# Decay masks of an SSD scan made by TensorE, with sums and products moved from POOL to DVE

## The chip, the cores and the metric

The kernel runs on one core of a Trainium2 chip. The metric is the device time of one execution in microseconds (us). Before the change it is 2617.65 us, the median of three runs (2610.93 to 2621.97).

The core has a matrix engine (PE in the profile, with its weight loads as PEld), a vector engine (DVE), an activation engine (ACT), a general engine (POOL) and a queue engine (SP), each of which works through its own list of instructions in order. [...] 

## The reference, cut to what matters

One encoder layer over 256 + 1024 tokens (1280 columns here), model width 1024, fp32. A projection gives the input of an S5 branch, of a bidirectional Mamba-2 (SSD) branch, and gates. Both branches are merged, projected, added to x, and a squared-ReLU MLP of width 4096 follows. The SSD branch has 24 heads of 64 in 4 groups, state 128, chunks of 128 tokens; it runs forward (d = 0) and backward (d = 1):

```python
da_cs = jnp.cumsum(dt * a, axis=2)                       # within a chunk
decay = jnp.exp(jnp.where(lower, da_cs[l] - da_cs[s], -jnp.inf))
cb = einsum('bclgn,bcsgn->bclsg', cm, bm)
y_diag = einsum('bclsg,bclsgk,bcsgkp->bclgkp', cb, decay, x * dt)
chunk_states = einsum('bcsgn,bcsgk,bcsgkp->bcgkpn', bm, decay_in, x * dt)
prev = scan: carry * chunk_decay + chunk_states
y_off = einsum('bclgn,bcgkpn,bclgk->bclgkp', cm, prev, jnp.exp(da_cs))
y = y_diag + y_off + d_skip * x;  out = rmsnorm_by_group(y * silu(z)) * w
```

For every pair (s, l) of a chunk and every head the kernel needs the weight dt[s] exp(cs[l] - cs[s]) in the lower triangle for one direction, in the upper for the other, times cb.

## The kernel before, in words

Activations lie with features on the partitions and the 1280 tokens along the free axis. Products of full precision are made as three fp32r matmuls (high and low parts of weights and inputs, mm3 at L129 and mm3n at L138) on 128x128 weight tiles over column chunks of 512, 512 and 256. Weights come over SP, are split by ACT (wh, L113) and POOL (wl, L114).

The order of the work on each engine is fixed when the kernel is built: a scheduler takes the instructions by priority (the order of the code, with parts marked urgent ahead) and by its own idea of when each is ready, and waits are then put in. So projection tiles that stand later in the code fill PE between the steps of earlier work.

The stages: input norm and projection of u; S5; the projection tiles EARLY (gates, conv and z tiles of group 0); dt_proc (L350 on); LATE (conv and z tiles of group 1); then the SSD with groups j = 0 to 3 and chunks k = 0 to 9, with the tiles of groups 2 and 3 and the last gates (TAIL) as fill; the GLU of S5; merge, output projection; MLP; final norm.

dt_proc computes dt (v), its sums within a chunk (e), and factors for the states (f) as 128x640 tiles (rows: half, direction, head). It writes e to the DRAM scratch cs_d in 16 stores and turns e, v and f by 15 PE transposes to per-token columns (ncs, dtt, dst).

chunk_in (L470) loads xf, transposes it (xt, L477), and advances the backward state (next_state, L447: POOL multiplies by dec, L454, PE makes the increment, L449, DVE adds, L456). chunk_out (L515) does one chunk of one group: SP loads bc and xz; PE makes cb (L523), DVE masks it twice (L525). ACT's queue loads ec, e broadcast over 64 partitions per head (L531), and ACT takes its exponential (L540); PE makes the off-diagonal products with the states (L538) in the banks ba and bk, DVE multiplies (L541), POOL adds the directions (L544). For each half of the six heads, ACT's queue loads cr, both directions' e broadcast over 128 partitions (L550); ACT subtracts the column's own e for direction 0 (L553), DVE does it for direction 1 and takes the minimum (L556), ACT takes the exponential (L558); ACT and DVE make the weight w of the two masked cb and dt (L561, L562), and DVE multiplies (L563). PE makes y (L568); DVE adds the skip (L571), POOL the off part and the gate (L573, L574); SP stores yt (L575); ACT squares (L578), POOL sums the squares (L579, L580).

PSUM in this stage: mm 2 banks, ps 2, ba 2, bk 1, y 1. The lines of the profile are those of the functions below.

Of the kernel before, what the change touches and what calls it, by code (L numbers as in the profile page):

```python
# [8 lines left out]
F32 = mybir.dt.float32  # L9
F32R = mybir.dt.float32r  # L10
I32 = mybir.dt.int32
AF = mybir.ActivationFunctionType
# [4 lines left out]
ADD, SUB, MUL, MIN, MAX = ALU.add, ALU.subtract, ALU.mult, ALU.min, ALU.max  # L17

P = 128
NT = 1280  # L20
# [6 lines left out]
HT = 640  # L27
# [1 line left out]
MC = 432  # L29
MAGIC = 12582912.0  # L30
NMM, NPA = 2, 6
PB = (2, 2, 1, 1)
PI = math.pi
TAU = 6.283185
GK = math.sqrt(2.0 / math.pi)
# [19 lines left out]
def tile_encoder(ctx: ExitStack, tc: tile.TileContext, a: dict, dbg=None):  # L55
    nc = tc.nc
    act, dve, pool, pe = nc.scalar, nc.vector, nc.gpsimd, nc.tensor

    cp = ctx.enter_context(tc.tile_pool(name="const", bufs=1))
    dr = ctx.enter_context(tc.tile_pool(name="scratch", bufs=1, space=DRAM))  # L60
# [18 lines left out]
    def C(n, i=0, w=None):  # L79
        o, ww = CST[n]  # L80
        return cst[:, o + i:o + i + (ww if w is None else w)]
# [5 lines left out]
    ident = C("ident")  # L87
# [9 lines left out]
    gate_d = dr.tile([16, P, NT], F32, name="gate_d")  # L97
    xbc_d = dr.tile([20, P, NT], F32, name="xbc_d")
    xz_d = dr.tile([4, 6, P, NT], F32, name="xz_d")
    cs_d = dr.tile([10, 4, 2, 6, P], F32, name="cs_d")  # L100

    def urgent():
        return tc.high_priority(offset=URG) if URG else ExitStack()
# [53 lines left out]
    with ExitStack() as pctx:  # L157
# [16 lines left out]
        with tc.tile_pool(name="xp0", bufs=1) as xp:  # L174
# [52 lines left out]
            for (c0, cn), x in zip(CH, xs):  # L227
                s = slice(c0, c0 + cn)
                for k in range(KD):
# [5 lines left out]
                    sq = xp.tile([P, 512], F32, name="sq", bufs=3)[:, :cn]  # L235
                    act.activation(sq, x[:, k], AF.Square)
                    dve.tensor_tensor(ss[:, s], ss[:, s], sq, ADD)
            with urgent():
# [4 lines left out]
                ms, r, t = (xp.tile([P, nb], F32, name=n) for n in ("ms1", "r1", "t1"))  # L243
# [88 lines left out]
        G = lambda i0, i1: [(gate_tile, i) for i in range(i0, i1)]  # L332
# [6 lines left out]
        EARLY, LATE, TAIL = G(0, 10) + X(0) + Z(0), X(1) + Z(1), G(10, 16)  # L339
        emit(EARLY)  # L340
        kp = pctx.enter_context(tc.tile_pool(name="ssdk", bufs=1))
        ncs, dtt, dst, dec = (kp.tile([P, 10, 48], F32, name=n) for n in ("ncs", "dtt", "dst", "dec"))

        def dt_proc():

            with tc.tile_pool(name="dtp", bufs=1) as dp:
                def T(n, dt=F32):
                    return dp.tile([P, HT], dt, name=n)
                v, e, n, f, q = (T(x) for x in ("dtv", "dte", "dtn", "dtf", "dtq"))
# [32 lines left out]
                for o in (e, f):  # L382
                    for r0 in (0, 32, 64, 96):
                        s = slice(r0, r0 + 32)
                        if (r0 % 64 == 32) == (o is e):
                            dve.tensor_tensor_scan(rv(o[s]), mk[s], rv(n[s]), 0.0, MUL, ADD)
                        else:
                            dve.tensor_tensor_scan(o[s], mk[s], n[s], 0.0, MUL, ADD)
                for h in range(2):
                    for j in range(4):  # L390
                        for d in range(2):
                            r = 64 * h + 32 * d + 6 * j
                            nc.sync.dma_start(cs_d[5 * h:5 * h + 5, j, d].rearrange("k r l -> r k l"),
                                              by_chunk(e[r:r + 6]))
                dve.tensor_tensor(f, f, n, SUB)
                act.activation(f, f, AF.Exp)
                dve.tensor_tensor(f, f, v, MUL)
# [2 lines left out]
                for r0 in (0, 32, 64, 96):  # L400
                    s = slice(r0, r0 + 32)
                    l = 127 if r0 % 64 == 0 else 0
# [6 lines left out]
                for k0, kn in ((0, 4), (4, 1)):  # L409
# [2 lines left out]
                              start=True, stop=True)  # L412
                    for h in range(2):
                        act.activation(halves(dec, k0, kn)[:, h], split_h(pt[:, :kn * P])[:, h], AF.Exp)
                for src, dst_, sg in ((e, ncs, -1.0), (v, dtt, 1.0), (f, dst, 1.0)):
                    for k0, kn in ((0, 4), (4, 1)):
                        pt = bank()
                        for k in range(kn):
                            pe.transpose(pt[:, k * P:(k + 1) * P], src[:, (k0 + k) * P:(k0 + k + 1) * P], ident)
                        for h in range(2):  # L420
                            act.activation(halves(dst_, k0, kn)[:, h], split_h(pt[:, :kn * P])[:, h], AF.Copy, scale=sg)
# [6 lines left out]
        def place(tag, bufs):  # L428
            return pq.tile([P, 512], F32, name=tag, bufs=bufs)
# [17 lines left out]
        def next_state(xt, xs, old, new, j, k, d):  # L447
            st = place("ps", PB[0])
            pe.matmul(st[:, :384], xt[:, 384:512], xs, start=True, stop=True)  # L449
            r = 24 * d + 6 * j  # L450
            if old is None:
                act.activation(new, st[:, :384], AF.Copy)
            else:
                pool.tensor_tensor(v6(new), v6(old),  # L454
                                   dec[:, k, r:r + 6].unsqueeze(2).to_broadcast([P, 6, 64]), MUL)
                dve.tensor_tensor(new, new, st[:, :384], ADD)  # L456

# [54 lines left out]
            rsqrt(nc, r, ms, t)  # L512
            nc.sync.dma_start(rs_d[j, k0:k0 + n], r)

        def chunk_out(j, k, xt, sf, sb, ssum):  # L515
            bc = sp.tile([P, 2, P], F32, name="bc")
            nc.sync.dma_start(bc, xbc_d[5 * j + 3:5 * j + 5, :, cols(k)].rearrange("m p l -> p m l"))
            xz = sp.tile([P, 6, P], F32, name="xz", bufs=2)
            nc.sync.dma_start(xz, xz_d[j, :, :, cols(k)].rearrange("m p l -> p m l"))
            sz, xd = xz[:, 0:3], xz[:, 3:6]  # L520
            bf, cf = bc[:, 0], bc[:, 1]
            ba = place("ba", PB[1])
            pe.matmul(ba[:, 384:512], bf, cf, start=True, stop=True)  # L523
            cb = sp.tile([P, 2, P], F32, name="cb")
            dve.tensor_tensor(cb, ba[:, 384:512].unsqueeze(1).to_broadcast([P, 2, P]),  # L525
                              C("low", 0, 2 * P).rearrange("p (i l) -> p i l", i=2), MUL)
            cbl, cbu = cb[:, 0], cb[:, 1]
            ec = sp.tile([P, 2, 3, P], F32, name="ec", bufs=2)
            rows = cs_d[k, j].rearrange("d (q e) l -> e d q l", e=2)
            for e0 in range(2):  # L530
                nc.scalar.dma_start(ec[e0 * 64:e0 * 64 + 64], rows[e0:e0 + 1].to_broadcast([64, 2, 3, P]))  # L531
            offs = []
            for d, st in ((0, sf), (1, sb)):
                if st is None:
                    continue
                bk = ba if not offs else place("bk", PB[2])
                for q in range(3):
                    pe.matmul(bk[:, q * P:(q + 1) * P], st[:, q * P:(q + 1) * P], cf, start=True, stop=True)  # L538
                ef = ec[:, d].rearrange("p q l -> p (q l)")
                act.activation(ef, ef, AF.Exp)  # L540
                dve.tensor_tensor(ef, ef, bk[:, 0:384], MUL)  # L541
                offs.append(ef)
            if len(offs) == 2:
                pool.tensor_tensor(offs[0], offs[0], offs[1], ADD)  # L544
            G = []
            for hh_ in range(2):
                e = sp.tile([P, 3, P], F32, name="e", bufs=4)
                w = sp.tile([P, 3, P], F32, name="w", bufs=2)
                cr = sp.tile([P, 2, 3, P], F32, name="cr", bufs=2)
                nc.scalar.dma_start(cr, cs_d[k, j, :, 3 * hh_:3 * hh_ + 3].unsqueeze(0).to_broadcast([P, 2, 3, P]))  # L550
                r = 6 * j + 3 * hh_
                for h in range(3):
                    act.activation(e[:, h], cr[:, 0, h], AF.Identity, bias=ncs[:, k, r + h:r + h + 1])  # L553

                for h in range(3):
                    dve.scalar_tensor_tensor(e[:, h], cr[:, 1, h], ncs[:, k, 24 + r + h:25 + r + h], e[:, h], ADD, MIN)  # L556
                ef = e.rearrange("p h l -> p (h l)")
                act.activation(ef, ef, AF.Exp)  # L558
                for h in range(3):
                    f, b = (dtt[:, k, 24 * d + r + h:24 * d + r + h + 1] for d in range(2))  # L560
                    act.activation(w[:, h], cbl, AF.Copy, scale=f)  # L561
                    dve.scalar_tensor_tensor(w[:, h], cbu, b, w[:, h], MUL, ADD)  # L562
                dve.tensor_tensor(e, e, w, MUL)  # L563
                G.append(e)
            y = place("y", PB[3])
            for h in range(6):
                q, e0 = divmod(h, 2)
                pe.matmul(y[e0 * 64:e0 * 64 + 64, q * P:(q + 1) * P], xt[:, h * 64:h * 64 + 64],  # L568
                          G[h // 3][:, h % 3], start=True, stop=True)
            yt = sp.tile([P, 384], F32, name="yt")  # L570
            dve.tensor_tensor(yt, y[:, :384], xd.rearrange("p q l -> p (q l)"), ADD)  # L571
            if offs:
                pool.tensor_tensor(yt, yt, offs[0], ADD)  # L573
            pool.tensor_tensor(yt, yt, sz.rearrange("p q l -> p (q l)"), MUL)  # L574
            nc.sync.dma_start(w_d[3 * j:3 * j + 3, :, cols(k)].rearrange("m p l -> p m l"),  # L575
                              yt.rearrange("p (q l) -> p q l", q=3))
            sq = sp.tile([P, 3, P], F32, name="sq", bufs=1)
            act.activation(sq.rearrange("p q l -> p (q l)"), yt, AF.Square)  # L578
            pool.tensor_tensor(sq[:, 0], sq[:, 0], sq[:, 1], ADD)  # L579
            pool.tensor_tensor(ssum, sq[:, 0], sq[:, 2], ADD)  # L580

        ins = [(j, k) for j in range(4) for k in (1, 0, 9, 8, 7, 6, 5, 4, 3, 2)]
        for j in range(4):
# [698 lines left out]
```

## Time and profile before

| | |
|---|---|
| median of 3 runs | 2617.65 us |
| the profiled execution | 2624.81 us, its span 2623.0 us, mean granted TensorE clock 0.979 |
| PE busy | 2461.0 us (94%), weight loads 2094.9 (80%) |
| DVE busy | 1578.7 us (60%) |
| ACT busy | 1052.0 us (40%) |
| POOL busy | 1011.3 us (39%) |
| chain of waits, by engine | PE 56%, DVE 20%, DMA 9%, ACT 5%, issue 5%, POOL 3% |
| HBM | 240.73 MB read, 72.52 MB written |

Busy time is the union of an engine's instructions. Matmuls are pipelined and their ends are modelled: one that starts alone shows some 0.4 us though the next can start 0.23 us after it. The chain of waits is followed back from the last instruction, at each step to what released it.

### The profile page before, as it was taken

How to read it: one execution, taken by the hardware profiler on the slowest of the kernel's cores; microseconds unless marked ns; L12 is line 12 of the kernel's file. 1: busy time of each engine (PE TensorE's matmuls, PEld its weight loads, DVE VectorE, ACT ScalarE, POOL GpSimd, SP SyncE). 2: the span in 40 equal slices, each digit the busy share in tenths (PEclk: the TensorE clock that was granted, in tenths of full speed). 3: DMA queues.
4: the chain of work that ended last, by engine and by line, in shares of the span. 5: the costliest groups of instructions: out<-in, count | busy, mean ns of one | idle time of the engine just before them, and what ended most of it. 6: DMA issues, size and time to landing. Idle time of an engine off the chain costs nothing.

```text
span 2623.0 us, 37529 instructions
## 1 busy us (share of the span) xinstructions
PE 2461.0 (94%) x13809; PEld 2094.9 (80%) x13809; DVE 1578.7 (60%) x2641; ACT 1052.0 (40%) x2308; POOL 1011.3 (39%) x790
## 2 busy tenths in 40 slices
PE   8899998798988999898899899999999999999998
PEld 6688877686866777676799898988888888888887
DVE  7799999786488786769752645433333333333336
ACT  7455555326566674666442434411111111111114
POOL 2511111122364553557644667632222232222235
PEclk9999999899999999998999999999999999999999
DMA  4323223226466665766556666531111111111113
GB/s 146 97 84 98 90 89 96 79 74 180 158 193 199 196 215 156 215 211 203 175 180 195 209 199 205 168 124 41 37 37 41 37 37 41 37 37 41 36 42 116
DMA packets 273656, 315.73 MB, mean 120 GB/s; under 512 B 30520, under 2 KB 206400, under 8 KB 273472
## 3 DMA queue, kind: packets, MB, share of 16 engines
q1 hardware_dynamic: 217984, 262.20, 32.1%
q10 hardware_dynamic: 55488, 51.13, 6.7%
q8 instruction: 109, 1.79, 0.3%
q14 instruction: 75, 0.61, 0.1%
HBM read 240.73 MB, written 72.52 MB: 119 GB/s over the span
## 4 chain that ended last, share of the span: by engine, by line
PE 56%; DVE 20%; DMA 9%; ACT 5%; issue 5%; POOL 3%; ACTq 0%; SPq 0%; DVEq 0%; POOLq 0%
PE pa L138 24%; PE mm L129 12%; PE pa L129 9%; PE mm L138 8%; DMA ec<-cs_d 3%; DMA cr<-cs_d 2%; POOL wl L114 2%; DVE ac L307 2%; DVE z L1127 1%; DVE z L1126 1%; DVE w L562 1%; DMA raw<-w_m 1%; PE ps L449 1%; PE y L568 1%; DMA wt<-w_d 1%
## 5 line engine op out<-in xcount | busy, mean ns | idle before, releaser
L114 POOL TENSOR_TENSOR wl<-raw,wh 128x512 fp32r<-128x512 f32 (+1 forms) x422 | 597.7, 1421 | 1317.6 <-ACT wh L113 1299.8
L113 ACT ACTIVATE wh<-raw 128x512 fp32r<-128x512 f32 (+1 forms) x422 | 258.1, 614 | 938.5 <-PE pa L138 523.0
L129 PE MATMUL mm<-hh,wl 128*128 128x512 f32 (+1 forms) x1272 | 472.5, 371 | 42.3 <-POOL wl L114 9.8
L129 PE MATMUL mm<-hl,wh 128*128 128x512 f32 (+1 forms) x1272 | 467.6, 368 | 0.1
L129 PE MATMUL mm<-hh,wh 128*128 128x512 f32 (+1 forms) x1272 | 467.5, 368 | 0.0
L129 PEld LDWEIGHTS mm<-hh,wl 128*128 128x128 f32 x1272 | 245.8, 193 | 88.6 <-POOL wl L114 14.5
L129 PEld LDWEIGHTS mm<-hl,wh 128*128 128x128 f32 x1272 | 246.1, 194 | 40.6 <-issue 1.8
L129 PEld LDWEIGHTS mm<-hh,wh 128*128 128x128 f32 x1272 | 245.4, 193 | 40.8 <-issue 3.6
L138 PE MATMUL pa<-hid,wh 128*128 128x512 f32 (+1 forms) x1008 | 254.6, 357 | 0.0
L750 DVE TENSOR_TENSOR acc<-acc,pa 128x512 f32<-128x512 f32 (+1 forms) x252 | 138.2, 594 | 140.5 <-PE pa L138 140.5
L138 PEld LDWEIGHTS pa<-hid,wh 128*128 128x128 f32 x1008 | 170.3, 188 | 29.8
L734 DVE SCALAR_TENSOR_TENSOR r<-pa,rs 128x512 f32<-128x512 f32 (+1 forms) x72 | 39.6, 596 | 230.0 <-PE pa L138 230.0
L129 PE MATMUL pa<-gx,wh 128*128 128x432 f32 (+1 forms) x576 | 158.5, 356 | 0.0
L138 PE MATMUL pa<-xnh,wl 128*128 128x512 f32 (+1 forms) x576 | 155.8, 357 | 0.0
L138 PE MATMUL pa<-xnl,wh 128*128 128x512 f32 (+1 forms) x576 | 155.0, 357 | 0.0
L138 PE MATMUL pa<-xnh,wh 128*128 128x512 f32 (+1 forms) x576 | 154.0, 357 | 0.0
L138 PE MATMUL pa<-hid,wl 128*128 128x512 f32 (+1 forms) x504 | 143.4, 355 | 0.0
L556 DVE SCALAR_TENSOR_TENSOR e<-cr,ncs,e 128x128 f32<-128x128 f32 x240 | 123.9, 562 | 28.6 <-ACT e L553 26.6
L562 DVE SCALAR_TENSOR_TENSOR w<-cb,dtt,w 128x128 f32<-128x128 f32 x240 | 116.0, 529 | 7.4 <-ACT w L561 7.4
L307 DVE SCALAR_TENSOR_TENSOR ac<-xpad,hcw,ac 128x1282 f32<-128x1282 f32 x60 | 100.8, 1679 | 21.8 <-ACT ac L305 21.5
L129 PEld LDWEIGHTS pa<-gx,wh 128*128 128x128 f32 x576 | 108.3, 188 | 3.6
L138 PEld LDWEIGHTS pa<-xnh,wh 128*128 128x128 f32 x576 | 96.5, 188 | 17.8
(449 smaller groups left out, 5071.7 us busy)
## 6 DMA issues: line engine op xcount, KB each, us to landing
cr<-cs_d ACTq DMA_DIRECT2D x80, 384.0 KB
raw<-w_in SPq DMA_DIRECT2D x110, 256.0 KB
raw<-w_m SPq DMA_DIRECT2D x72, 256.0 KB
raw<-w_dn SPq DMA_DIRECT2D x72, 256.0 KB
raw<-w_up SPq DMA_DIRECT2D x64, 256.0 KB
ec<-cs_d ACTq DMA_DIRECT2D x80, 192.0 KB
xz<-xz_d SPq DMA_DIRECT2D x40, 384.0 KB
raw<-w_o SPq DMA_DIRECT2D x48, 256.0 KB
```

Of the source, the lines that this page charges most:

```text
L113: act.activation(wh[:, :n], raw[:, :n], AF.Copy)
L114: pool.tensor_tensor(wl[:, :n], raw[:, :n], wh[:, :n], SUB)
L129: pe.matmul(out, l, r[:, sl], start=(n == 0), stop=(n == last))
L138: pe.matmul(o, l, r[:, sl], start=(n == 0), stop=(n == last))
L307: dve.scalar_tensor_tensor(ac[:, :n], xp[:, k:k + n], w(k), ac[:, :n], MUL, ADD)
L449: pe.matmul(st[:, :384], xt[:, 384:512], xs, start=True, stop=True)
L556: dve.scalar_tensor_tensor(e[:, h], cr[:, 1, h], ncs[:, k, 24 + r + h:25 + r + h], e[:, h], ADD, MIN)
L562: dve.scalar_tensor_tensor(w[:, h], cbu, b, w[:, h], MUL, ADD)
L568: pe.matmul(y[e0 * 64:e0 * 64 + 64, q * P:(q + 1) * P], xt[:, h * 64:h * 64 + 64], G[h // 3][:, h % 3], start=True, stop=True)
L734: dve.scalar_tensor_tensor(r[:, s], pt, 0.0, rs2[:, s], MAX, MUL)
L750: dve.tensor_tensor(ac[:, m, s], ac[:, m, s], pt, ADD)
L1126: dve.tensor_tensor_scan(z[lo, 2:n + 2], flat(dk)[lo], flat(src)[lo], 0.0, MUL, ADD)
```

## The change

dt_proc writes e itself to es_d, and in high and low parts (two fp32r numbers that add up to it) to cs_d; log(dt) - e goes to ns_d in the same way. The transposes of e and v and the tiles ncs and dtt go. In the SSD, chunk_loads brings bc, ec, the rows er and el, and xz, all on SP and one chunk ahead. For each half of the heads and each direction PE writes a mask (0 or -1e30) into PSUM with the identity as weights, and adds the exponents cs[l] + log dt[s] - cs[s] with a matmul of 16 rows (el: two rows of ones for cs and the parts of ns; er: the parts of cs, and ones that pick the head). One exponential of 768 columns on ACT serves both directions; DVE adds them and multiplies by cb, which ACT copies out of PSUM. Products and sums on POOL in next_state and chunk_out go to DVE. ba gets one bank, bk is replaced by y's, and ex gets two banks with one buffer.

```diff
-PB = (2, 2, 1, 1)
+PB = (2, 1, 1, 1)
+BIG = 1.0e30
...
-    cs_d = dr.tile([10, 4, 2, 6, P], F32, name="cs_d")
...
+    cs_d = dr.tile([4, 2, 2, 6, NT], F32, name="cs_d")
+    es_d = dr.tile([4, 2, 6, NT], F32, name="es_d")
+    ns_d = dr.tile([4, 2, 6, 2, NT], F32, name="ns_d")
...
-        ncs, dtt, dst, dec = (kp.tile([P, 10, 48], F32, name=n) for n in ("ncs", "dtt", "dst", "dec"))
+        dst, dec = (kp.tile([P, 10, 48], F32, name=n) for n in ("dst", "dec"))
...
+                def parts(src, dst_):
+                    hl2 = [T(f"{src.name}p{i}", F32R) for i in range(2)]
+                    act.activation(hl2[0], src, AF.Copy)
+                    dve.tensor_tensor(hl2[1], src, hl2[0], SUB)
+                    for i in range(2):
+                        for h in range(2):
+                            for d in range(2):
+                                r = 64 * h + 32 * d
+                                nc.sync.dma_start(dst_(i, d)[:, :, h * HT:h * HT + HT], hl2[i][r:r + 24].bitcast(F32))
...
-                    for j in range(4):
...
-                                              by_chunk(e[r:r + 6]))
+                    for d in range(2):
+                        r = 64 * h + 32 * d
+                        nc.sync.dma_start(es_d[:, d, :, h * HT:h * HT + HT], e[r:r + 24])
+                parts(e, lambda i, d: cs_d[:, d, i])
+                dve.tensor_scalar(q, v, 1e-37, None, MAX)
+                act.activation(q, q, AF.Ln)
+                dve.tensor_tensor(q, q, e, SUB)
+                parts(q, lambda i, d: ns_d[:, d, :, i])
...
-                for src, dst_, sg in ((e, ncs, -1.0), (v, dtt, 1.0), (f, dst, 1.0)):
+                for src, dst_, sg in ((f, dst, 1.0),):
...
-                pool.tensor_tensor(v6(new), v6(old),
+                dve.tensor_tensor(v6(new), v6(old),
...
-        def chunk_out(j, k, xt, sf, sb, ssum):
...
+        NR = 2
+        ers = [sp.tile([16, 6, P], F32R, name=f"er{i}", bufs=1) for i in range(NR)]
+        els = [sp.tile([16, 2, P], F32R, name=f"el{i}", bufs=1) for i in range(NR)]
+        for i in range(NR):
+            B6 = [16, 6, P]
+            pick = lambda o: ident[0:16, 4 + o:16 + o:2].unsqueeze(2).to_broadcast(B6)
+            dve.tensor_tensor(ers[i], pick(0), pick(1), ADD)
+            for d in range(2):
+                dve.tensor_tensor(els[i][:, d], *(ident[0:16, c:c + 1].to_broadcast([16, P]) for c in (2 * d, 2 * d + 1)), ADD)
...
+        eye = sp.tile([P, P], F32R, name="eye", bufs=1)
+        dve.tensor_copy(eye, ident)
+        out_of = sp.tile([P, 2, P], F32R, name="out_of", bufs=1)
+        dve.tensor_scalar(out_of.rearrange("p i l -> p (i l)"), C("low", 0, 2 * P), BIG, BIG, MUL, SUB)
+        nth = [0]
...
+        def chunk_loads(j, k):
+            i = nth[0] % NR
+            nth[0] += 1
+            er, el = ers[i], els[i]
...
-            xz = sp.tile([P, 6, P], F32, name="xz", bufs=2)
+            ec = sp.tile([P, 2, 3, P], F32, name="ec")
+            rows = es_d[j, :, :, cols(k)].rearrange("d (q e) l -> e d q l", e=2)
+            for e0 in range(2):
+                nc.sync.dma_start(ec[e0 * 64:e0 * 64 + 64], rows[e0:e0 + 1].to_broadcast([64, 2, 3, P]))
+            nc.sync.dma_start(er[0:4].bitcast(F32), cs_d[j].rearrange("d i r t -> (d i) r t")[:, :, cols(k)])
+            nc.sync.dma_start(el[4:16].bitcast(F32), ns_d[j, :, :, :, cols(k)].rearrange("d r i l -> (r i) d l"))
+            xz = sp.tile([P, 6, P], F32, name="xz")
...
+            return bc, xz, ec, er, el
...
+        order = [(j, k) for j in range(4) for k in range(10)]
+        ahead = {}
...
+        def chunk_out(j, k, xt, sf, sb, ssum):
+            i = 10 * j + k
+            for z in order[i:i + 2]:
+                if z not in ahead:
+                    ahead[z] = chunk_loads(*z)
+            bc, xz, ec, er, el = ahead.pop((j, k))
...
-            cb = sp.tile([P, 2, P], F32, name="cb")
...
-                nc.scalar.dma_start(ec[e0 * 64:e0 * 64 + 64], rows[e0:e0 + 1].to_broadcast([64, 2, 3, P]))
+            cb = sp.tile([P, 1, P], F32, name="cb")
+            act.activation(cb[:, 0], ba[:, 384:512], AF.Copy)
...
-                bk = ba if not offs else place("bk", PB[2])
+                bk = ba if not offs else place("y", PB[3])
...
-                pool.tensor_tensor(offs[0], offs[0], offs[1], ADD)
+                dve.tensor_tensor(offs[0], offs[0], offs[1], ADD)
...
-                e = sp.tile([P, 3, P], F32, name="e", bufs=4)
...
-                G.append(e)
+                ps = pq.tile([P, 2, 512], F32, name="ex", bufs=1)[:, :, :384]
+                for d in range(2):
+                    pe.matmul(ps[:, d].rearrange("p (h l) -> p h l", h=3), eye, out_of[:, d:d + 1].to_broadcast([P, 3, P]),
+                              start=True, stop=False)
+                    pe.matmul(ps[:, d], el[:, d], er[:, 3 * hh_:3 * hh_ + 3].rearrange("p h l -> p (h l)"),
+                              start=False, stop=True)
+                e = sp.tile([P, 2, 384], F32, name="e", bufs=3)
+                act.activation(e, ps, AF.Exp)
+                dve.tensor_tensor(e[:, 0], e[:, 0], e[:, 1], ADD)
+                ev = e[:, 0].rearrange("p (h l) -> p h l", h=3)
+                dve.tensor_tensor(ev, ev, cb.to_broadcast([P, 3, P]), MUL)
+                G.append(ev)
...
-                pool.tensor_tensor(yt, yt, offs[0], ADD)
-            pool.tensor_tensor(yt, yt, sz.rearrange("p q l -> p (q l)"), MUL)
+                dve.tensor_tensor(yt, yt, offs[0], ADD)
+            dve.tensor_tensor(yt, yt, sz.rearrange("p q l -> p (q l)"), MUL)
...
-            pool.tensor_tensor(sq[:, 0], sq[:, 0], sq[:, 1], ADD)
-            pool.tensor_tensor(ssum, sq[:, 0], sq[:, 2], ADD)
+            dve.tensor_tensor(sq[:, 0], sq[:, 0], sq[:, 1], ADD)
+            dve.tensor_tensor(ssum, sq[:, 0], sq[:, 2], ADD)
...
```

## Rows read from the trace of the kernel before

**Rows 1.** Busy time by stretch: us, busy us (x instructions) per engine, clock, DMA share, GB/s.

```profile
core 0: us, PE busy (x) PEld busy (x) DVE busy (x) ACT busy (x) POOL busy (x), PEclk, DMA share, GB/s
570.00:600.00 30.00, 26.01 (x129) 20.95 (x127) 26.66 (x27) 9.36 (x16) 4.23 (x3) 1.00 0.23 69
600.00:1240.00 640.00, 583.72 (x3247) 464.52 (x3247) 471.53 (x907) 411.53 (x1093) 321.37 (x307) 0.97 0.65 195
1240.00:1370.00 130.00, 113.60 (x729) 106.71 (x730) 86.42 (x120) 56.32 (x117) 81.48 (x66) 0.96 0.58 178
1700.00:2560.00 860.00, 860.00 (x4405) 726.37 (x4405) 297.03 (x488) 123.13 (x163) 242.36 (x162) 1.00 0.14 46
```

**Rows 2.** Chain of waits, 600 to 1240 us, share of the stretch by line.

```profile
by line: PE mm L129 27.5%; DMA ec<-cs_d 10.4%; DMA cr<-cs_d 8.2%; issue 8.0%; DVE w L562 4.8%; DVE ac L307 3.5%; PE ps L449 3.3%; PE y L568 2.8%; DVE e L556 1.9%; DMA xz_d<-ac 1.8%; ACT e L553 1.8%; POOL yt L573 1.7%; ACT ac L305 1.5%; ACT 
```

**Rows 3.** TensorE's waits, 570 to 1370: who for whom, us, times, longest.

```profile
PE y L568 <- DVE e L563: 10.0, 10, 2.7
PE ps L449 <- ACT xs L440: 9.5, 3, 5.7
PE mm L129 <- ACT xpad L301: 7.5, 3, 4.3
PE ba L523 <- DMA bc<-xbc_d: 6.1, 4, 2.0
...
PE ba L538 <- DVE cb L525: 0.2, 1, 0.2
...
PEld y L568 <- issue: 11.5, 29, 1.9
```

**Rows 4.** Timeline, TensorE's matmuls back to back: start, us, what.

```profile
899.94 0.39 PE L129 MATMUL mm<-hh,wl 128*128 128x512 f32 x1
900.17 0.39 PE L129 MATMUL mm<-hl,wh 128*128 128x512 f32 x1
...
909.52 0.28 PE L129 MATMUL mm<-hl,wh 128*128 128x256 f32 x1
909.64 0.28 PE L129 MATMUL mm<-hh,wh 128*128 128x256 f32 x1
```

**Rows 5.** DVE, groups of instructions (busy us, mean ns); lines (ns min/median/max).

```profile
L556 DVE SCALAR_TENSOR_TENSOR e<-cr,ncs,e 128x128 f32<-128x128 f32 x240 | 123.9, 562 | 28.6 <-ACT e L553 26.6 <-DMA xz<-xz_d 1.7
L562 DVE SCALAR_TENSOR_TENSOR w<-cb,dtt,w 128x128 f32<-128x128 f32 x240 | 116.0, 529 | 7.4 <-ACT w L561 7.4
...
L556 DVE SCALAR_TENSOR_TENSOR e<-cr,ncs,e x240: 330/348/1387, 613.7 to 1261.8; 128x128 f32<-128x128 f32 x120
...
L571 DVE TENSOR_TENSOR yt<-y,xz x40: 537/545/558, 647.9 to 1270.2; 128x384 f32<-128x384 f32 x40
```

**Rows 6.** POOL, a group and a line, as rows 5.

```profile
L573 POOL TENSOR_TENSOR yt<-yt,ec 128x384 f32<-128x384 f32 x40 | 46.5, 1164 | 64.8 <-DVE yt L571 41.6 <-DVE ec L541 19.1 <-issue 3.1
...
L544 POOL TENSOR_TENSOR ec<-ec x24: 994/1050/5872, 723.9 to 1258.2; 128x384 f32<-128x384 f32 x24
```

**Rows 7.** ACT, groups and lines, as rows 5.

```profile
L553 ACT ACTIVATE e<-cr,ncs 128x128 f32<-128x128 f32 x240 | 77.8, 391 | 26.7 <-DMA cr<-cs_d 18.9 <-PE y L568 3.2 <-PE mm L129 3.1
L561 ACT ACTIVATE w<-cb,dtt 128x128 f32<-128x128 f32 x240 | 75.6, 389 | 12.7 <-DVE e L563 10.3 <-DVE cb L525 1.9
...
L480 ACT ACTIVATE xt<-ps x40: 572/580/599, 621.8 to 1179.9; 128x512 f32<-128x512 f32 x40
...
L452 ACT ACTIVATE sf<-ps x8: 467/476/492, 698.3 to 1186.5; 128x384 f32<-128x384 f32 x8
```

**Rows 8.** Queues: ec's issue, and waits of ACT and SP, 600 to 1240.

```profile
L531 ACTq DMA_DIRECT2D ec<-cs_d x80: 581/608/1302, 602.2 to 1256.1; - x80
...
ACT ec L540 <- DMA ec<-cs_d: 48.7, 26, 3.7
...
SPq L575 <- POOL yt L574: 144.7, 32, 13.5
SPq L112 <- POOL wl L114: 82.8, 37, 10.9
```

**Rows 9.** DVE, one difference of 128x640 in dt_proc.

```profile
L395 DVE TENSOR_TENSOR dtf<-dtf,dtn 128x640 f32<-128x640 f32 x1 | 0.8, 826 | 0.0
```

More of the change, by code (lines that the diff above doesn't have):

```diff
@@ L388, in dt_proc @@
                             dve.tensor_tensor_scan(o[s], mk[s], n[s], 0.0, MUL, ADD)
-                for h in range(2):
-                    for j in range(4):
-                        for d in range(2):
-                            r = 64 * h + 32 * d + 6 * j
-                            nc.sync.dma_start(cs_d[5 * h:5 * h + 5, j, d].rearrange("k r l -> r k l"),
-                                              by_chunk(e[r:r + 6]))
+                def parts(src, dst_):
[7 more added lines that the diff above has]
+                                nc.sync.dma_start(dst_(i, d)[:, :, h * HT:h * HT + HT], hl2[i][r:r + 24].bitcast(F32))
+                for h in range(2):
+                    for d in range(2):
[6 more added lines that the diff above has]
+                parts(q, lambda i, d: ns_d[:, d, :, i])
                 dve.tensor_tensor(f, f, n, SUB)
@@ L523, in chunk_out @@
             pe.matmul(ba[:, 384:512], bf, cf, start=True, stop=True)
-            cb = sp.tile([P, 2, P], F32, name="cb")
[L525 to L530, printed above, removed]
-                nc.scalar.dma_start(ec[e0 * 64:e0 * 64 + 64], rows[e0:e0 + 1].to_broadcast([64, 2, 3, P]))
+            cb = sp.tile([P, 1, P], F32, name="cb")
+            act.activation(cb[:, 0], ba[:, 384:512], AF.Copy)
             offs = []
@@ L543, in chunk_out @@
             if len(offs) == 2:
-                pool.tensor_tensor(offs[0], offs[0], offs[1], ADD)
+                dve.tensor_tensor(offs[0], offs[0], offs[1], ADD)
             G = []
             for hh_ in range(2):
-                e = sp.tile([P, 3, P], F32, name="e", bufs=4)
[L548 to L563, printed above, removed]
-                G.append(e)
+                ps = pq.tile([P, 2, 512], F32, name="ex", bufs=1)[:, :, :384]
[10 more added lines that the diff above has]
+                G.append(ev)
             y = place("y", PB[3])
```

## The prediction

> **What bounds the kernel now.** I read the busy time by stretch first, then the chain of waits for the stretch that the change touches, then what TensorE waits for there. The reader is to see three things.
>
> First, in the MLP stretch (1700 to 2560 us) PE is busy all of 860 us, while DVE, ACT and POOL stand at 14 to 35%: PE alone sets the time. In the SSD stretch (600 to 1240 us) PE is busy 583.7 of 640 us, DVE 471.5, ACT 411.5, POOL 321.4 [rows 1]. So PE is close to full there too, because projection, gate and GLU matmuls (L129) are put between the SSD's own.
>
> Second, busy time hides bubbles. The weight loads show them: 726.4 of 860 us in the full stretch (0.845), 464.5 of 640 (0.726) in the SSD stretch, so the SSD stretch runs at 0.726 / 0.845 = 86% of the rate of a full PE [rows 1]. Headroom is 56 us by PE's idle time and 0.14 x 640 = 90 us by the weight loads.
>
> Third, the chain through the SSD stretch is not mainly PE: 27.5% is L129, 18.6% (119 us) is the landing of ec and cr, and the rest DVE, ACT and POOL pieces [rows 2]. PE runs out of fill in short spells and then waits for one of these. The waits themselves are small and many: 27 groups in 570 to 1370 us, from 10.0 us (ten waits for e) down to 0.2 [rows 3].
>
> The argument is therefore a balance: the change puts work on the engine that is nearly full, and shortens the chain that keeps it from being full.
>
> **The change part by part.**
>
> *PE, added.* 40 chunks x 2 halves x 2 directions x 2 matmuls = 320 fp32r matmuls of 384 columns (mask, then exponents). Back to back, fp32r matmuls of 512 columns start 0.23 us apart and those of 256 columns 0.12 us [rows 4]; halfway is 0.176 us, so 320 x 0.176 = 56 us. Bounds: 0.12 and 0.235 give 38 and 75. That one of each pair has 16 rows only I price like a full one, as no row shows fewer rows. Removed are 10 transposes at about 0.1 us (from starts of five in a row): 1 us, left out.
>
> *DVE.* Gone: L556 123.9 and L562 116.0 us, 240 in all (and the masking of cb, which I leave out). The product L563 stays (with the broadcast cb instead of w). Added: 80 sums of 384 at 0.545, the median of L571, which has that size, = 44; from POOL 152 operations of 384 (40 each of L573 and L574, 24 of L544, 48 of L454) = 83, and 80 of 128 (L579, L580) at 0.33, the fastest L556, = 26. Net 153 - 240 = -87 us [rows 5, 6]. DVE goes from 472 to some 385 of 640 us; it is no bound in either kernel. What counts is that a chunk's DVE path shortens.
>
> The spread in row L556 matters: 330 ns at best, median 348, mean 562, maximum 1387, while L571, which reads PSUM, stays within 537 to 558 [rows 5]. Something holds up DVE operations with two SBUF operands; POOL's own maximum on L544 (5.9 us with a median of 1.05) says that it works both ways [rows 6]. [...] In the sum I use medians from these rows anyway.
>
> *POOL.* Some 220 us go, 46.5 of them on L573, and about as much on L574 [rows 6]. Its waits cost the chain little directly; what it delays is SP: the store of yt holds the SP queue 144.7 us in this stretch, with later loads behind it [rows 8].
>
> *ACT.* Gone: L553 77.8 and L561 75.6 = 153 us, and 80 exponentials of 384 columns. Added: 80 exponentials of 768 columns from PSUM; 384 take 0.476 and 512 take 0.580, so 0.580 + 2 x 0.104 = 0.79; and 40 copies of cb at 0.39, as L553. Each exponential costs 0.79 - 0.48 = 0.31 more: 25 + 16 - 153 = -112 us [rows 7]. Its queue also loses 160 issues (80 of ec at 0.61 = 49 us, and 80 of cr), and its 48.7 us of waiting for ec mostly go, since ec is now loaded one chunk (some 16 us: 622 us between the first and last of 40 yt) ahead of use [rows 5, 8]. ACT's load in the stretch, 412 busy + 49 issuing + 49 waiting of 640, becomes about 300. It evacuates the fill's banks too, so this is where I expect most of what PE gets back.
>
> *SP.* 160 issues are added (80 ec, 40 er, 40 el); at up to 0.61 us that is up to 97 us [rows 8] on a queue that mostly stands in waits. What stands behind a blocked load is weight loads and stores. I price it at 0, covered by the chunk of lead; without that cover it is a rival below.
>
> *dt.* Two high and low splits (a copy on ACT and a difference on DVE each), a max, a logarithm, one more difference, all of 128x640, where one takes 0.83 us, and 20 instead of 16 stores: 7 operations in line make 6 us before the first chunk, 10 with the stores [rows 9]. PE has the LATE tiles as fill: 8 tiles x 72 matmuls x 0.195 = 112 us of work, and it is busy 26 of 30 us there [rows 1]. Price 0; 10 us if LATE were already spent.
>
> *PSUM.* ps stays at two banks, y also serves the second off product, ex takes two banks and one buffer. So PE's matmuls for the second half wait until ACT has read the first. New handoffs: 80. A restart of PE after a handoff for which the trace names no releaser costs 11.5 us for 29 of them at y, 0.4 each [rows 3]; not every handoff shows it (29 of the 40 chunks at y). Bounds 0 and 80 x 0.4 = 32; I take 12 (0.15 each), nearer to the lower end since most handoffs meet fill.
>
> *What PE gets back.* Of its waits those released by ACT, DMA or POOL in the SSD: xs 9.5, xpad 7.5, bc 6.1 and six smaller, together 37 us: taken whole. Released by DVE (e 10.0 to cb 0.2, eight groups): 24, half taken, since POOL's operations now stand in the same queue: 12 [rows 3]. The granted clock is 0.97 in the stretch and 1.00 in the full one [rows 1]: 0.03 x 640 = 19 us at most, paid where PE stood idle before; a quarter taken: 5. [...]
>
> Sum: +56 + 12 - 37 - 12 - 5 = **+14 us**. The profiled execution took 2624.8 us (span 2623.0), so 2639 on its terms; the median of the runs shown is 2617.65, 7 us lower, so **2632**.
>
> **Rivals.**
>
> *PE fills up (faster).* If all waits of the stretch go, PE's 90 us of headroom take the added 56 and 34 are left: 2617.65 - 34 = 2584; with two thirds of the headroom recovered and no new bubbles it breaks even, so the middle is about 2600. For it: 18.6% of the chain is loads that are now a chunk early, and ACT loses almost half its load. Against: the stretch 1240 to 1370, with few SSD pieces, still has 16 us of idle PE in 130 [rows 1]. [...] Chance 0.30.
>
> *The single ex buffer (much slower).* The place is PE's queue between the first and the second half of a chunk: where no fill was placed there, PE stands for one exponential, 0.80 us plus a handoff of 0.2. All 80 exposed cost 80 us, half of them 40: 2632 + 40 = 2672. It decides from the point where over a third of them are exposed. For it: y and ba have one buffer each as well. Against: L129 is 58% of the stretch's matmuls, so fill is there. Chance 0.18.
>
> *SP's order (slower).* ec now stands behind weight loads, which hold SP up to 10.9 us, and yt's stores, up to 13.5 us [rows 8]. That is within the lead of 16 us; if both come in one chunk, ACT waits as before and the 15 or so us that I gave back for it are lost: 2647. Chance 0.05.
>
> *Likeliest.* PE-bound with part of the waits gone, 2605 to 2655. Chance 0.47.
>
> **How the numbers follow.** Half a percent (13 us) is about what a measurement of this kernel can tell from no change. Below 2604.6: nearly all of the first rival (0.29) and the low edge of the likeliest (0.03), 0.32. Within: 0.23 of the likeliest and 0.01, 0.24. Above 2630.7: 0.21 and the other two (0.23), 0.44. The range reaches from the first rival's full gain to the second with 58 of its 80 exponentials exposed: 2584 to 2690.
>
> **What would show it.** PE's matmuls in the SSD stretch rise by 320 and its busy share goes above 0.93, weight loads above 0.78 of the time; the PE waits on xs, xpad and bc fall under a third; the new exponential's row reads 0.75 to 0.85 us; L563's product and the new DVE rows 0.53 to 0.6 with little spread; the idle time of PE before the ex matmuls stays under 20 us in all. The prediction is wrong if the ex matmuls step faster than 0.15 or slower than 0.2 us, if PE's idle time is not reduced at all, or if the stretch ends over 25 us earlier than now although PE's work rose.

## The result and the profile after

The changed kernel takes 2657.12 us (median of four, 2649.95 to 2661.94) against 2616.35 us before on the same chips: ratio 1.0144, 95% interval [1.0124, 1.0164], 38 us slower. (The two medians lie 41 us apart; the text goes by the ratio.) The forecast was 2632, so the sign is right and the size is not: 38 us where 14 were expected. In all these kernels SP and ACT's queue issue the transfers (DMA).

Busy time of the changed kernel by stretch, columns as in [rows 1]:

```profile
core 0: us, PE busy (x) PEld busy (x) DVE busy (x) ACT busy (x) POOL busy (x), PEclk, DMA share, GB/s
570.00:600.00 30.00, 19.37 (x91) 15.94 (x91) 22.61 (x31) 12.19 (x23) 4.67 (x2) 0.84 0.44 132
600.00:1240.00 640.00, 638.95 (x3383) 477.91 (x3381) 377.12 (x685) 292.15 (x627) 109.07 (x85) 1.00 0.45 138
1240.00:1370.00 130.00, 117.69 (x723) 105.04 (x723) 81.66 (x123) 53.51 (x101) 56.04 (x43) 0.93 0.63 195
1700.00:2560.00 860.00, 860.00 (x4417) 730.33 (x4416) 300.36 (x490) 130.48 (x180) 250.96 (x170) 1.00 0.15 49
```

The whole profiled execution (2649.95 us): span and clock, and from its page the busy time (us, share of the span, instructions):

```profile
core 0: 2648.2 us, clock 0.987
...
PE 2545.5 (96%) x14119; PEld 2132.3 (81%) x14119; DVE 1494.1 (56%) x2445; ACT 948.4 (36%) x1864; POOL 792.3 (30%) x558
```

In the SSD stretch PE is now busy 638.95 of 640 us at a granted clock of 1.00, as in the MLP. DVE, ACT and POOL are where the prediction put them (377, 292, 109). So PE's idle time in this stretch is gone, and the kernel is slower all the same. Its chain of waits, 600 to 1280 us, share by line, against [rows 2]:

```profile
by line: PE mm L133 55.1%; PE ex L600 8.5%; PE ps L466 6.6%; PE ex L598 6.3%; PE y L611 5.8%; PE ba L587 4.2%; PE ps L494 2.6%; PE y L587 2.4%; PE ps L525 1.5%; PE ba L578 1.5%; DMA ec<-es_d 1.0%; DVE ac L311 0.8%; DMA bc<-xbc_d 0.8%; DMA x
```

It is TensorE almost throughout: L129 has become L133, and 14.8% of it, 101 us of 680, are the new matmuls into ex. TensorE's waits, 570 to 1370, answer to [rows 3] (who for whom, us, times, longest):

```profile
PE ex L598 <- DMA xz_d<-ac: 8.2, 1, 8.2
PE mm L133 <- DVE t L699: 6.2, 4, 2.8
PE mm L133 <- DVE sx5l L155: 2.7, 1, 2.7
PE pa L428 <- DVE dg L422: 2.4, 1, 2.4
PE mm L133 <- ACT sx5h L154: 2.0, 1, 2.0
PE ex L598 <- ACT e L603: 0.9, 1, 0.9
```

Of the waits for e, xs, xpad and bc 0.3 us is left (xpad), and the feared wait of ex for the exponential is 0.9 us in all. One new wait is big: 8.2 us just before 600 us, where the first mask matmul stands in PE's queue until DVE, behind a convolution's steps, has made the constants that it reads. The view names a transfer as the releaser, but the last of the constants is done 0.2 us before the matmul starts:

```profile
595.24 0.27 DVE L547 TENSOR_SCALAR out_of<-cst 128x256 fp32r<-128x256 f32 x1
...
595.73 0.66 PE L598 MATMUL ex<-out_of,eye 128*128 128x384 f32 x1 [8.20 <-DMA xz_d<-ac]
```

The price is in the ex matmuls themselves. One half chunk, matmuls and then weight loads (start, us, what, idle before):

```profile
806.13 0.34 PE L598 MATMUL ex<-out_of,eye 128*128 128x384 f32 x1
806.40 0.44 PE L600 MATMUL ex<-er,el 16*128 16x384 f32 x1
806.77 0.44 PE L598 MATMUL ex<-out_of,eye 128*128 128x384 f32 x1
807.14 0.44 PE L600 MATMUL ex<-er,el 16*128 16x384 f32 x1
807.51 0.50 PE L133 MATMUL mm<-hh,wh 128*128 128x512 f32 x1
807.85 0.40 PE L133 MATMUL mm<-hh,wl 128*128 128x512 f32 x1
...
805.89 0.19 PEld L598 LDWEIGHTS ex<-out_of,eye 128*128 128x128 f32 x1
806.39 0.18 PEld L600 LDWEIGHTS ex<-er,el 16*128 16x128 f32 x1 [0.32 <-issue]
806.76 0.19 PEld L598 LDWEIGHTS ex<-out_of,eye 128*128 128x128 f32 x1 [0.19 <-issue]
807.13 0.18 PEld L600 LDWEIGHTS ex<-er,el 16*128 16x128 f32 x1 [0.18 <-issue]
807.50 0.19 PEld L133 LDWEIGHTS mm<-hh,wh 128*128 128x128 f32 x1 [0.19 <-issue]
807.61 0.19 PEld L133 LDWEIGHTS mm<-hh,wl 128*128 128x128 f32 x1
```

The first step is 0.27 us and the other three are 0.37, not 0.176. The weight loads tell why: before the first ex matmul it starts 0.24 us ahead of its matmul, under the one before; before the next four it starts 0.01 us ahead and its matmul waits for it. That is so at every change between 128 and 16 rows in this trace (the 160 loads of 16 rows all start 0 to 0.01 us ahead of their matmul), the way back to the projection included (next step 0.34 for 0.23). A half chunk takes 1.38 us and another 0.11 behind it; 80 of them 119 us, where I had put 56.

### The profile page after: what moved, and what is told of

It reads as the page before. It is cut to its first block, busy times and chain, and to the rows that moved or that the text cites. A ratio compares the mean times of both kernels' runs of the same rounds, so it can differ in the third digit from the quotient of the medians.

```text
span 2648.2 us, 37077 instructions
## 1 busy us (share of the span) xinstructions
PE 2545.5 (96%) x14119; PEld 2132.3 (81%) x14119; DVE 1494.1 (56%) x2445; ACT 948.4 (36%) x1864; POOL 792.3 (30%) x558
## 4 chain that ended last, share of the span: by engine, by line
PE 72%; DVE 17%; DMA 4%; ACT 3%; issue 2%; POOL 1%; SPq 0%; DVEq 0%; ACTq 0%; POOLq 0%
PE pa L142 24%; PE mm L133 20%; PE pa L133 9%; PE mm L142 8%; PE ex L600 2%; PE ps L466 2%; PE ex L598 2%; PE y L611 2%; DMA wt<-w_d 1%; DVE z L1170 1%; DVE z L1169 1%; DVE ac L311 1%; PE ba L587 1%; POOL wl L118 1%; PE ps L494 1%
## 5 line engine op out<-in xcount | busy, mean ns | idle before, releaser
L118 POOL TENSOR_TENSOR wl<-raw,wh 128x512 fp32r<-128x512 f32 (+1 forms) x422 | 590.2, 1403 | 1604.1 <-ACT wh L117 1516.8
L133 PE MATMUL mm<-hh,wl 128*128 128x512 f32 (+1 forms) x1272 | 470.1, 370 | 22.5 <-ACT hh L220 7.4
L133 PE MATMUL mm<-hh,wh 128*128 128x512 f32 (+1 forms) x1272 | 468.5, 368 | 0.0
L133 PE MATMUL mm<-hl,wh 128*128 128x512 f32 (+1 forms) x1272 | 466.5, 367 | 0.0
L133 PEld LDWEIGHTS mm<-hh,wl 128*128 128x128 f32 x1272 | 242.8, 191 | 67.9 <-issue 10.1
L133 PEld LDWEIGHTS mm<-hl,wh 128*128 128x128 f32 x1272 | 243.0, 191 | 43.6 <-issue 6.7
L133 PEld LDWEIGHTS mm<-hh,wh 128*128 128x128 f32 x1272 | 242.8, 191 | 42.6 <-issue 6.4
L133 PE MATMUL pa<-gx,wh 128*128 128x432 f32 (+1 forms) x576 | 158.6, 356 | 0.0
L133 PEld LDWEIGHTS pa<-gx,wh 128*128 128x128 f32 x576 | 108.4, 188 | 3.5
L142 PEld LDWEIGHTS pa<-xnh,wl 128*128 128x128 f32 x576 | 96.6, 188 | 17.8
L142 PEld LDWEIGHTS pa<-xnl,wh 128*128 128x128 f32 x576 | 96.4, 188 | 17.9
```

Source lines behind the costliest of these rows:

```text
L118: pool.tensor_tensor(wl[:, :n], raw[:, :n], wh[:, :n], SUB)
L133: pe.matmul(out, l, r[:, sl], start=(n == 0), stop=(n == last))
L142: pe.matmul(o, l, r[:, sl], start=(n == 0), stop=(n == last))
```

## The experiments

Ratios are to the kernel before, with the 95% interval; differences between two experiments are those of their ratios times 2620 us. The first four shared a chip, so did early_setup, mask_dve, pool_back and no_lead, and the last two.

**rows128**, er and el on all rows, those from 16 on zero:

```diff
-        ers = [sp.tile([16, 6, P], F32R, name=f"er{i}", bufs=1) for i in range(NR)]
-        els = [sp.tile([16, 2, P], F32R, name=f"el{i}", bufs=1) for i in range(NR)]
+        ers = [sp.tile([P, 6, P], F32R, name=f"er{i}", bufs=1) for i in range(NR)]
+        els = [sp.tile([P, 2, P], F32R, name=f"el{i}", bufs=1) for i in range(NR)]
...
-            pick = lambda o: ident[0:16, 4 + o:16 + o:2].unsqueeze(2).to_broadcast(B6)
+            pick = lambda o: ident[0:P, 4 + o:16 + o:2].unsqueeze(2).to_broadcast(B6)
...
```

> The changed kernel with er and el on all 128 rows (rows 16 to 127 zero), so that all matmuls of the mask and the exponents use the same rows. Theory A (a matmul of 16 rows beside one of 128 keeps the next weight load from running under the current matmul, about 0.19 us each time): the 384-column matmuls step 0.176 us as the first of each four does now, four of them take 0.70 instead of about 1.3 us plus 0.19 before the next projection matmul; 80 x 0.77 = 60 us less, about 2597 us, faster than the kernel before. Theory B (accumulating into a bank just written, or the exponents' operand itself, makes the step 0.37 us): no change, 2657. Theory C (128 rows take longer than 16): over 2657.

Measured 2617.59 us, 0.9981 [0.9965, 0.9997]: 43 us under the changed kernel. The timeline of a half chunk (start, us, what):

```profile
904.17 0.39 PE L133 MATMUL mm<-hh,wh 128*128 128x512 f32 x1
904.40 0.34 PE L598 MATMUL ex<-out_of,eye 128*128 128x384 f32 x1
904.58 0.34 PE L600 MATMUL ex<-er,el 128*128 128x384 f32 x1
904.75 0.35 PE L598 MATMUL ex<-out_of,eye 128*128 128x384 f32 x1
904.94 0.34 PE L600 MATMUL ex<-er,el 128*128 128x384 f32 x1
905.12 0.39 PE L133 MATMUL mm<-hh,wl 128*128 128x512 f32 x1
905.35 0.40 PE L133 MATMUL mm<-hl,wh 128*128 128x512 f32 x1
```

Four take 0.72 us, 58 us for 80, and the next step is 0.23. Theories B and C fall: the same accumulation into the same banks steps at 0.18 once all rows are used. The time stays 20 us above the 2597 that theory A gave it: of the 61 us that PE saves, 18 come back as idle time. PE is busy 621.8 of 640 us in the stretch, not 639.

**masks_first**:

```diff
                     pe.matmul(ps[:, d].rearrange("p (h l) -> p h l", h=3), eye, out_of[:, d:d + 1].to_broadcast([P, 3, P]),
                               start=True, stop=False)
+                for d in range(2):
                     pe.matmul(ps[:, d], el[:, d], er[:, 3 * hh_:3 * hh_ + 3].rearrange("p h l -> p (h l)"),
                               start=False, stop=True)
```

> The changed kernel with the two mask matmuls of 128 rows first and the two of 16 rows behind them. Theory A: the number of changes between row counts in a half chunk falls from four (128 to 16, to 128, to 16, to 128) to two, so 80 x 2 x 0.19 = 30 us less, about 2627. Theory B (each accumulating matmul and the one behind it are slow): the 16-row matmuls stay at 0.37 us each and the second mask falls to 0.176, so 15 us less at most, 2642. With neither, 2657.

Measured 2639.71, 1.0066 [1.0041, 1.009]: 20 us less than the changed kernel. Half chunks (start, us, what, two at a time):

```profile
703.90 0.51 PE L598 MATMUL ex<-out_of,eye 128*128 128x384 f32 x2
704.34 0.62 PE L601 MATMUL ex<-er,el 16*128 16x384 f32 x2
704.88 0.50 PE L133 MATMUL mm<-hl,wh 128*128 128x512 f32 x1
```

Two 16-row matmuls take 0.54 us where two of 128 rows take 0.35; at B's price they would take 0.74. The total is nearer to B's 2642 than to A's 2627, but it is the timeline that decides, as idle time comes back here too.

**rows64**, the same edit with 64:

> The changed kernel with er and el on 64 rows. Theory A in its form 'any difference in row count': steps of 0.37 us as with 16 rows, 2657. Theory A in the form 'only the smallest row counts': steps of 0.176, about 2597.

Measured 2659.01, 1.0139 [1.0108, 1.017]: no gain over 16 rows. Its matmuls of 64 rows (ns min/median/max) last as long as those of 16 rows, whose median is 439 too:

```profile
L600 PE MATMUL ex<-er,el x160: 435/439/443, 618.4 to 1280.3; 64*128 64x384 f32 x160
```

So it is not the smallness: 64 rows beside 128 cost what 16 cost. Other row counts were not tried.

**moves_only**, the kernel before with `pool.tensor_tensor` as `dve.tensor_tensor` at L454, L544, L573, L574, L579 and L580:

> The kernel before with only the six kinds of POOL sums and products in next_state and chunk_out on DVE. If POOL and DVE holding each other up is what makes TensorE wait: DVE's 128x128 operations with two SBUF operands fall from a mean of 562 ns towards their median of 348, and the time falls by 10 to 25 us, to 2592 to 2606. If the waits came from ACT and the loads: within 8 us of 2616. If DVE becomes the bound (472 busy of 640 us plus 109): slower, over 2630.

Measured 2590.99, 0.9881 [0.9859, 0.9903]: 31 us faster, more than any theory gave it. DVE's groups (busy, mean ns), beside [rows 5]:

```profile
L556 DVE SCALAR_TENSOR_TENSOR e<-cr,ncs,e 128x128 f32<-128x128 f32 x240 | 82.6, 378 | 16.0 <-ACT e L553 16.0
L562 DVE SCALAR_TENSOR_TENSOR w<-cb,dtt,w 128x128 f32<-128x128 f32 x240 | 82.1, 382 | 8.2 <-ACT w L561 7.6 <-ACT xpad L301 0.4
```

The means fall from 562 and 529 to 378 and 382 ns with no edit to these lines, as POOL's busy time from 600 to 1240 falls from 321 [rows 1] to 149 us: POOL's work had been holding them up. By what mechanism is not shown, nor that the 31 us come from this alone. The edit also shortens the chunk's own path (the two operations on yt take 660 and 606 ns on DVE, 1164 and 1244 on POOL), and the store of yt holds SP's queue for 25.7 us behind L574 instead of 144.7 [rows 8]; no run takes these apart.

**pool_back**, rows128 with those six back on POOL:

> rows128 with the six kinds of sums and products back on POOL, so of the change the TensorE exponents, loads and single exponential alone. If the moves are worth the same here as alone (31 us): 2649. If the exponents had taken the same waits away already: 2618 to 2630. If the exponents alone are the loss and the moves the whole gain: over 2645.

Measured 2620.6, 0.9998 [0.9985, 1.0011], within the error of rows128 (0.9981). So the second theory: with the exponents on PE the moves are worth some 4 us, alone 31, so the two edits take away the same waits. POOL's work still costs DVE time here (a 384 product takes 833 ns, 675 in rows128), but DVE has idle time to pay with:

```profile
L606 DVE TENSOR_TENSOR e<-e,cb 128x384 f32<-128x384 f32 x80 | 66.4, 833 | 1.8
L604 DVE TENSOR_TENSOR e<-e 128x384 f32<-128x384 f32 x80 | 61.8, 773 | 105.9 <-ACT e L603 105.7
```

**no_lead**, rows128 with `order[i:i + 1]` for `order[i:i + 2]`:

> rows128 with each chunk's loads issued in its own chunk instead of one ahead. If the lead is what ends ACT's waits for ec: TensorE's waits rise by 15 to 25 us, 2633 to 2643. If issuing on SP instead of ACT's queue is enough: within 5 us of 2617.6.

Measured 2620.17, 0.9989 [0.9974, 1.0004]: the second theory. The lead of a chunk is worth nothing that shows. I had credited it with ending ACT's waits for ec, but these grew: 48.7 us from 600 to 1240 before, 85.3 in the changed kernel, 108.0 in rows128 and 104.9 here. TensorE's waits in the changed kernel name none of them.

**early_setup**, rows128 with er, el, eye and out_of made ahead of dt_proc:

> rows128 with the constants (er, el, eye, out_of) made by DVE ahead of dt_proc, not behind LATE's first convolution. If TensorE's 6.6 us of waiting at the first mask matmul and the lower clock behind it (10 us at half) are paid by the whole: 2606, 11 us under rows128's 2617.6. If that time is given back because dt_proc, which runs on DVE, ends 3 us later and fill is short there: 2612 to 2618.

Measured 2619.17, 0.9993 [0.9975, 1.0011], no gain. Its waits of TensorE:

```profile
PE mm L133 <- ACT sx5h L154: 5.5, 1, 5.5
...
PE ex L598 <- ACT dst L452: 3.9, 1, 3.9
```

The wait at the first mask falls from 6.6 to 3.9 us, now behind dt_proc's last copies, and the GLU waits 5.5 us for sx5h, 1.9 in rows128 (but 5.0 in pool_back, which lacks this edit). That the 3 us of work ahead of dt_proc is what took the rest back was not shown.

**mask_dve**, the version without the mask matmuls:

```diff
-                    pe.matmul(ps[:, d].rearrange("p (h l) -> p h l", h=3), eye, out_of[:, d:d + 1].to_broadcast([P, 3, P]),
-                              start=True, stop=False)
...
-                              start=False, stop=True)
+                              start=True, stop=True)
...
-                act.activation(e, ps, AF.Exp)
+                for d in range(2):
+                    dve.tensor_tensor(e[:, d].rearrange("p (h l) -> p h l", h=3), ps[:, d].rearrange("p (h l) -> p h l", h=3),
+                                      out_of[:, d:d + 1].to_broadcast([P, 3, P]), ADD)
+                act.activation(e, e, AF.Exp)
```

> rows128 without the mask matmuls; DVE adds the mask while it brings the exponents from PSUM to SBUF (two additions of 384 columns a half chunk, 0.55 us each, 88 us in all), ACT takes the exponential from SBUF. If TensorE's own work sets the time: 160 x 0.176 = 28 us less, 2590. If the longer way over DVE (1.1 us more in every half chunk, one ex buffer) brings waits back: 2605 to 2625.

Measured 2586.49, 0.9861 [0.9837, 0.9885]: 31 us under rows128 for 28 us of PE's work taken away, and the lowest of all versions, though its interval overlaps that of moves_only. DVE's new additions (busy, mean ns) are busy time that hides:

```profile
L602 DVE TENSOR_TENSOR e<-ex,out_of 128x384 f32<-128x384 f32 x160 | 81.8, 547 | 15.1 <-PE ex L598 14.9
```

**mask_dve16**, the same with er and el on 16 rows:

> mask_dve with er and el on 16 rows again: two 16-row matmuls in a row between work of 128 rows. If a change of the row count costs one uncovered weight load (0.19 us) and equal neighbours cost nothing: two changes a half chunk, 80 x 2 x 0.19 = 30 us more, less what falls into TensorE's waits, so 2606 to 2617; and of each pair the first steps 0.37 and the second 0.176 us. If 16 rows were slow by themselves: both 0.37.

Measured 2606.04, 0.9938 [0.9915, 0.996]: 20 us more than mask_dve, at the lower edge of what was expected. The pair and what follows it (start, us, what):

```profile
699.62 0.40 PE L133 MATMUL mm<-hl,wh 128*128 128x512 f32 x1
699.95 0.61 PE L598 MATMUL ex<-er,el 16*128 16x384 f32 x2
700.49 0.50 PE L133 MATMUL mm<-hh,wh 128*128 128x512 f32 x1
700.83 0.39 PE L133 MATMUL mm<-hh,wl 128*128 128x512 f32 x1
...
699.95 0.29 PEld L598 LDWEIGHTS ex<-er,el 16*128 16x128 f32 x2 [0.37 <-issue]
700.49 0.19 PEld L133 LDWEIGHTS mm<-hh,wh 128*128 128x128 f32 x1 [0.25 <-issue]
```

The first start is 0.33 us behind a 512-column matmul instead of 0.23, the two take 0.54 instead of 0.35, and the 512-column matmul behind them steps 0.34 instead of 0.23. That is 0.40 us more in all, about two loads of 0.19: one for the way in, one for the way out. Between equals there is none: both 16-row loads are through within 0.29 us, the second under the first matmul. The steps of 0.37 and 0.176 expected within the pair are not there (0.54 for both): of the 0.40 us, 0.10 falls on the step ahead of the pair, 0.19 on the pair and 0.11 on the step behind it. This shows the cost of the change of rows without any mask or accumulation.

**moves_sp**, moves_only with `nc.sync` for `nc.scalar` at the loads of ec and cr:

> moves_only with the loads of ec and cr issued on SP instead of ACT's queue. ACT loses 160 issues of 0.37 to 0.61 us (78 us). If ACT's queue is what still makes TensorE wait (xs 11.6, xpad): 2575 to 2585. If SP's order, with weight loads and stores ahead of ec and cr, takes it back: 2591 or more.

Measured 2594.0, 0.9886 [0.9863, 0.9909], the same as moves_only. TensorE's waits, 570 to 1370, in moves_only:

```profile
PE ps L449 <- ACT xs L440: 11.6, 5, 6.3
...
PE ba L523 <- DMA bc<-xbc_d: 2.6, 1, 2.6
PE bk L538 <- DMA bc<-xbc_d: 2.3, 1, 2.3
```

and here:

```profile
PE ba L523 <- DMA bc<-xbc_d: 17.3, 8, 4.3
...
PE ps L449 <- ACT xs L440: 0.9, 1, 0.9
```

The time goes by the second theory, and these rows show how: with ACT's queue free the waits for xs go (10.7 us), and the waits for bc, whose loads now share SP's queue with ec and cr, grow by as much (12.4 us).

## Why the prediction was wrong

*The frame held, the balance did not.* The change puts work on an engine that is nearly full, and the price of that work on PE decides the time; DVE, ACT and POOL cost nothing that shows. But the sign came out right by luck. With the ex matmuls at the price forecast (rows128, 58 us for 56) the kernel is 5 us faster than before, where the same balance forecast it 14 slower. What made it slower is a cost that the prediction did not have.

*The step that failed* is "PE, added": "That one of each pair has 16 rows only I price like a full one, as no row shows fewer rows." The term of 56 us measured 119 (80 x 1.49), beyond its upper bound of 75. The bounds came from column counts, and the unknown lay in the rows: what a change of row count does to the next weight load. rows128 takes it away (1.38 to 0.72 us a half chunk), mask_dve16 brings it back. The mark set beforehand, wrong if the ex matmuls step slower than 0.2 us, was met.

*"What PE gets back"* was too small: 37 + 12 + 5 = 54 us, less 12 for handoffs. With 119 us added and 38 lost, 81 came back; with 58 added and 5 won (rows128), 63. The handoffs cost next to nothing (0.9 us of waiting). This is the mechanism of the first rival: nearer to the weight loads' 90 us of headroom than to the 56 us of idle time [rows 1] came back. Idle time alone does not make it up: over the whole execution PE's idle time falls from 162.0 (2623.0 - 2461.0) to 102.7 us (2648.2 - 2545.5), by 59. The two profiled executions lie 25 us apart, so 119 - 25 = 94 us came back in them, and 35 of these are PE's busy time, in which the rest of its work got denser. The clock of the stretch (0.97 before, 1.00 after) may be a part of that; no run shows it. With the right price of the ex matmuls and all 90 us back the sum would have been 119 - 90 = 29 us, near the 38. The two mis-sized terms, +63 and -39, go opposite ways; the forecast was off by their difference.

*Whose waits they were* was also read too simply. I gave them out by the engine that the row names: ACT's to the loads and to ACT's issues, a half of DVE's to DVE. no_lead shows that the lead is worth nothing, and moves_sp that freeing ACT's queue wins one wait and loses another. By moves_only, taking the SSD's sums and products off POOL, which is named as releaser for under 7 us of PE's waits, is worth 31.

*dt:* a price of 0 with 10 as the other end. PE did stand for 8.2 us there, at a clock of 0.84 in that stretch; early_setup did not win it back, so what it cost in the end stays open.

*The new DVE rows* were forecast at 0.53 to 0.6 us with little spread. The medians fit, 0.557 and 0.552 us for the sum and the product (L604, L606), but the means are 0.610 and 0.660 and the longest take 1.65 and 1.67. POOL is still busy 109 us in the stretch; whether that is the reason was not tested.

*Right:* the single ex buffer and SP's order cost nothing that shows; the exponential takes 0.805 us (0.79 forecast); PE is busy above 0.93. Weight loads stay at 0.747 of the time, under the 0.78 that I named, because uncovered loads take PE's time without filling it; in rows128 they are 507 of 640, 0.79.

## What to carry to other kernels

Where an engine is nearly full, price added work on it by its own form, rows as well as columns; where no row has that form, the bounds must include a weight load per matmul (0.19 us here), not only the streaming time. Give small operands of a matmul the full 128 rows, with zeros, if its neighbours have them; here that won 43 us. What several edits give back comes out of one pot: the moves alone gave back 31 us (moves_only), the exponents on PE alone the 58 that they cost (pool_back takes as long as the kernel before), and both together 63 (rows128). So try each alone: moves_only, at 2590.99 us, puts nothing on PE, and the best kernel with the exponents on PE, mask_dve at 2586.49, is not clearly below it.

## What the runs showed of the hardware

Of the row counts tried here, a weight load ran under the matmul before it only where both used the same number of rows. 16 rows beside 128 cost some 0.19 us at each change (a 384-column step of 0.37 us in the changed kernel, 0.18 in rows128), 64 beside 128 as much (matmuls with a median of 439 ns at 16 and 64 rows, 337 at 128). 128 beside 128 cost nothing (rows128), 16 behind 16 nothing (mask_dve16: both loads through in 0.29 us). DVE's 128x128 operations at L556 lost a third of their mean time (562 to 378 ns) when POOL's sums and products of the SSD left (moves_only), though only the mean moved: the medians were 348 and 341.
